# Block 2: two pairs of value projections of each layer as seven half products instead of eight

## The chip, the cores and the metric

The kernel runs on one core of a Trainium2 chip. Its measure is the device time of one execution: median 2514.1 us of three runs, from 2513.4 to 2515.23. The engines are PE (matrix multiply), DVE (vector), ACT (scalar), POOL (GpSimd) and SP, which here only issues DMAs. Each engine takes its instructions in the order written, and waits on semaphores for the others.

## The reference, cut to what matters

Two blocks run on 512 tokens of width 1024: the first ends with a feed-forward net (ffn), the second has two layers of which each computes

```
mod = c_act @ w_ada + b_ada                       # shift, scale, gate
h = rmsnorm(x, norm_w) * (1 + scale) + shift      # 512 x 1024
qa, ka, va, za, qr, kr, vr, zr, ga, gr = split(h @ w_in)
# attention: 3 patterns of 4 heads of 128; patterns 1 and 2 take keys by stride 4 and 16
o_att = softmax-weighted sum over the 3 patterns;  y_att = o_att * silu(za)
o_ret = retention(qr, kr, vr, positions);           y_ret = o_ret * silu(zr)
merged = sigmoid(ga) * (y_att @ w_proj_attn) + sigmoid(gr) * (y_ret @ w_proj_ret)
x = x + gate * (merged @ w_out)
```

va is 512 x 1536, 512 columns for each pattern; vr is 512 x 1024. The change is in how the columns of va for patterns 1 and 2, and both halves of vr, are computed from h. All is in 32-bit floats. A product of two such matrices is done as three matmuls on split operands: each matrix is kept as a high part (`h`, `wh`) and a low part (`l`, `wl`, the rest), and hi·hi, hi·lo and lo·hi are summed in PSUM.

## The kernel before

The work is one long list of TensorE matmuls of 128x128 by 128x512, and all else is arranged to have its operands there in time. A weight comes in pieces of 512 KB (128 partitions x 1024, two row blocks of 128 by 512 columns): `load_w` (L188) issues the DMA on SP into a raw tile `wr` (2 places), ACT rounds it to the high part `wh` (L144), DVE subtracts to get the low part `wl` (L145); `wh` and `wl` have 4 places each (5 where a second pool is given). A piece serves 24 matmuls: 2 row blocks, 4 blocks of 128 tokens, 3 terms. Loads are moved ahead in the instruction list by a priority offset, so SP's order is that of the loads with stores and other DMAs between them.

In block 2 `attention_v` (L959) makes the values of pattern 0 first (block of tokens by block, as soon as the norm has delivered them), and then, called inside `attention`, of patterns 1 and 2: four pieces of weight each into four PSUM banks, a copy by ACT, and 16 DMAs of 64 KB (L975) that spread each 128 tokens over four tiles by stride. The query and key projections of the 4 heads follow (`in_w_qk`), and their weights are loaded while the values are computed. `retention_v` (L1141) does the same for one half of vr, without DMAs: half 0 before retention, half 1 in its middle. `rotary_tables` (sines and cosines on DVE and ACT, L930 to L956) runs beside the first layer's strided values.

The merge loop (`rt2`, in the layer's main function) alternates weights of w_g and w_proj_ret; w_out follows. In the ffn stage a background task (`ada`) computes the modulation from 96 pieces of w_ada with DVE. Background tasks are generators: `tick()` after each group of matmuls advances them, and a number they yield is how many ticks to wait.

POOL works in the first 500 us and not after.

Of the kernel before, what the change touches and what calls it, by code (L numbers as in the profile page):

```python
# [15 lines left out]
P = 128  # L16
# [34 lines left out]
class Block:  # L51
# [136 lines left out]
    def load_w(self, src, into=None):  # L188
        with self.tc.high_priority(offset=50):
            raw = self.wp.tile([P, 1024], F32, tag="wr", name=self.nm("wr"), bufs=2)  # L190
            self.nc.sync.dma_start(out=raw, in_=src)
            if into is not None:
                self.split(*into, raw)
                return into
            self.nw += 1
            wp, n = (self.wx, 1) if self.wx and self.nw % 5 == 0 else (self.wp, 4)
            wh = wp.tile([P, 1024], F32R, tag="wh", name=self.nm("wh"), bufs=n)
            wl = wp.tile([P, 1024], F32R, tag="wl", name=self.nm("wl"), bufs=n)
            self.split(wh, wl, raw)
        return wh, wl  # L200
# [107 lines left out]

    def room(self, x):

        return [tuple(y[:, 2 * i:2 * i + 2, :].rearrange("p k q -> p (k q)") for y in (x.hi, x.lo)) for i in range(4)]
# [85 lines left out]
    def block1(self):  # L397
# [10 lines left out]
        self.nw, self.wx = 0, None  # L408
        self.wp = op(self.es, "w")
# [329 lines left out]
    def ffn(self, hf, fp, es_w):  # L739
# [5 lines left out]
        def done(i, ps):  # L745
            if i == 0:
# [4 lines left out]
                self.spawn(self.ada(pool[0], 1.2))  # L751
            if i % 2 == 0:
# [70 lines left out]
    def block2(self, h, es_w):  # L823
# [6 lines left out]
        for l in range(2):  # L830
# [7 lines left out]
            V = self.attention_v(l, h, vp, range(1))  # L838
            self.wait()
            es_w.close()  # L840
            mp, e_m = op("mrg", "right")
            mrg = [mp.tile([P, S], F32, tag="m", name=self.nm("m"), bufs=8) for _ in range(8)]
            with tc.tile_pool(name="att", bufs=1, side="right", reuse_waits="tile") as ap:
                if l == 0:
                    self.rotary_tables(ap)
                self.attention(l, h, ap, vp, V, ya, mrg)
            e_v.close()
            with tc.tile_pool(name="retv", bufs=1, side="right", reuse_waits="tile") as rv:
                W = self.retention_v(l, h, rv, 0)
# [12 lines left out]
            with tc.tile_pool(name="rt2", bufs=1, side="right", reuse_waits="tile") as rp:  # L862
                T = {}
                for i in range(11):
# [5 lines left out]
                    if c >= 0:  # L870
# [3 lines left out]
                        self.split(m.hi[:, c, :], m.lo[:, c, :], mrg[c], scale=0.5)  # L874
            e_m.close()
# [82 lines left out]

    def attention_v(self, l, h, vp, gs, V=None, ap=None):  # L959

        V = {} if V is None else V
        for g in gs:
            if g:
                for c in range(4):
                    V[g, c] = vp.tile([P, 512], F32, tag="V", name=self.nm("V"), bufs=12)

            def done(t, ps):
                if g == 0:
                    V[g, t] = vp.tile([P, 512], F32, tag="V", name=self.nm("V"), bufs=12)
                    self.nc.scalar.activation(V[g, t], ps, AF.Copy)  # L970
                    return
                x = ap.tile([P, 512], F32, tag="qk", name=self.nm("Vt"), bufs=4)
                self.nc.scalar.activation(x, ps, AF.Copy)
                for c in range(4):
                    self.nc.sync.dma_start(out=V[g, c][t * 32:t * 32 + 32, :], in_=x[c:P:4, :])  # L975

            self.T_(self.tok(h), self.A["w2_va"][l, g], 8, done, outer=0 if g else 4, ready=None if g else h.ready)
        return V

    def attention(self, l, h, ap, vp, V, ya, mrg):  # L980
# [141 lines left out]
        self.attention_v(l, h, vp, (1, 2), V, ap)  # L1122
        for hd in range(4):
            head(hd, range(3))
        self.spawn(finish(list(self.tasks)))
# [15 lines left out]
    def retention_v(self, l, h, rv, half):  # L1141
        V = []

        def done(t, ps):
            vt = rv.tile([P, 2, 512], F32R, tag="V", name=self.nm("V"), bufs=4)
            self.split(vt[:, 0, :], vt[:, 1, :], ps)
            V.append(vt)

        self.T_(self.tok(h), self.A["w2_vr"][l, half], 8, done, outer=2)
        return V  # L1150

    def retention(self, l, h, rp, rv, V, yr):
# [83 lines left out]
        Vs[1] = self.retention_v(l, h, rv, 1)  # L1236
# [417 lines left out]
```

## Time and profile before

| | us |
|---|---|
| median of 3 runs (2513.4 to 2515.23) | 2514.1 |
| profiled execution | 2515.06 |
| its span | 2513.3 |
| PE busy in the span | 2493.3 |
| DVE, ACT, POOL busy | 1403.6, 1062.7, 99.2 |

The profiled execution took 2515.06 us, of which 2513.3 lie in the span that the trace covers. The granted clock of PE is 1.0 throughout, its upper level. Approximate stages: ffn 820 to 1165 us; first layer of block 2: values 1165 to 1244, attention to 1445, values for retention to 1470, retention to 1690, merge to 1790, w_out to 1840; second layer: values to 1930, attention to 2130, and so on to the end. A view by windows says how busy each engine was in such a stage; a timeline gives single instructions with their start and length; the waits of SP are those of its DMA-issuing instructions.

### The profile page before, as it was taken

What the parts mean: (1) busy time and instruction counts of PE and PEld (TensorE: products, weight loads), DVE (VectorE), ACT (ScalarE), POOL (GpSimd) and SP (SyncE); (2) the same over time, 40 slices, a digit from 0 to 9 for tenths busy, and PEclk for the clock granted to TensorE, in tenths of its full rate; (3) what the DMA queues carried; (4) which work ended last, traced back from release to release, by engine and by line L of the source; (5) the groups of instructions that cost most, each with busy time, mean ns of one, the idle gap of its engine ahead of it and who ended that gap; (6) DMA issues with size and microseconds to landing.
All of it is one profiled execution on the core that took longest, in us unless ns stands there. A gap on an engine that the chain in (4) does not pass through costs nothing.

```text
span 2513.3 us, 31228 instructions
## 1 busy us (share of the span) xinstructions
PE 2493.3 (99%) x11850; PEld 2056.5 (82%) x11850; DVE 1403.6 (56%) x2651; ACT 1062.7 (42%) x1829; POOL 99.2 (4%) x104
## 2 busy tenths in 40 slices
PE   9999999999999999999999999999999999999998
PEld 7877777878888888888888888888888888888887
DVE  6567665776656777626333436664452343375635
ACT  4477666875334333324343432323233334233323
POOL 0023332000000000000000000000000000000000
PEclk9999999999999999999999999999999999999999
DMA  5522222323345666534422122222443222322233
GB/s 181 173 80 78 70 71 93 95 88 110 118 131 182 211 194 216 184 132 142 134 93 92 62 90 82 86 76 92 144 141 126 89 79 68 101 70 98 68 100 118
DMA packets 99129, 286.47 MB, mean 114 GB/s; under 512 B 13193, under 2 KB 19209, under 8 KB 98850
## 3 DMA queue, kind: packets, MB, share of 16 engines
q1 hardware_dynamic: 98256, 283.22, 35.2%
q8 instruction: 93, 1.52, 0.3%
q10 hardware_dynamic: 722, 1.25, 0.1%
q14 instruction: 58, 0.48, 0.1%
HBM read 259.16 MB, written 12.61 MB: 108 GB/s over the span
## 4 chain that ended last, share of the span: by engine, by line
PE 92%; DVE 3%; ACT 2%; DMA 2%; issue 1%; POOL 0%; ACTq 0%; POOLq 0%; DVEq 0%
PE ps L129 89%; PE ps L138 3%; DMA wr<-in_w_out_dram 1%; DVE wl L145 1%; ACT S L1416 1%; ACT wh L144 0%; DMA wr<-in_w_o_dram 0%; DVE yr L145 0%; POOL S L1423 0%; DVE PTl L145 0%; DVE S L1410 0%; ACT S L1421 0%; DMA x<-in_x_dram 0%; DVE xc L629 0%; DMA wr<-in_nsa_wv_dram 0%
## 5 line engine op out<-in xcount | busy, mean ns | idle before, releaser
L129 PE MATMUL ps<-h,wh 128*128 128x512 f32 (+1 forms) x4000 | 1242.8, 391 | 0.0
L129 PEld LDWEIGHTS ps<-h,wh 128*128 128x128 f32 x4000 | 733.5, 188 | 139.3 <-issue 5.1
L145 DVE TENSOR_TENSOR wl<-wr,wh 128x1024 fp32r<-128x1024 f32 x383 | 469.1, 1225 | 556.1 <-ACT wh L144 555.2
L144 ACT ACTIVATE wh<-wr 128x1024 fp32r<-128x1024 f32 x383 | 405.6, 1059 | 871.4 <-PE ps L129 658.3
L129 PE MATMUL ps<-h,wl 128*128 128x512 f32 (+1 forms) x2000 | 772.9, 386 | 0.0
L129 PEld LDWEIGHTS ps<-h,wl 128*128 128x128 f32 x2000 | 375.9, 188 | 75.7 <-DVE wl L145 0.4
L129 PE MATMUL ps<-wh,h 128*128 128x512 f32 x832 | 261.2, 392 | 0.3 <-ACT h L144 0.3
L129 PEld LDWEIGHTS ps<-wh,h 128*128 128x128 f32 x832 | 156.6, 188 | 33.6 <-DVE h L145 0.8
L129 PE MATMUL ps<-wl,h 128*128 128x512 f32 x416 | 162.4, 390 | 0.0
L129 PE MATMUL ps<-y,wh 128*128 128x512 f32 x384 | 119.3, 391 | 0.0
L129 PEld LDWEIGHTS ps<-wl,h 128*128 128x128 f32 x416 | 78.4, 188 | 16.1
L129 PE MATMUL ps<-wh,f 128*128 128x512 f32 x288 | 89.6, 389 | 0.0
L129 PEld LDWEIGHTS ps<-y,wh 128*128 128x128 f32 x384 | 71.5, 188 | 14.4
L129 PE MATMUL ps<-yr,wh 128*128 128x512 f32 x256 | 78.8, 389 | 0.0
L1416 ACT ACTIVATE S<-S,sm 128x128 f32<-128x128 f32 (+3 forms) x128 | 70.2, 550 | 19.0 <-DVE sm L1414 18.8
L1423 POOL TENSOR_SCALAR S<-S,sm 128x128 f32<-128x128 f32 (+3 forms) x64 | 69.6, 1099 | 214.0 <-ACT Q L144 78.2
L145 DVE TENSOR_TENSOR PTl<-ps,PTh 128x512 fp32r<-128x512 f32 (+1 forms) x96 | 65.0, 683 | 22.4 <-ACT PTh L144 21.6
L144 ACT ACTIVATE PTh<-ps 128x512 fp32r<-128x512 f32 (+1 forms) x96 | 56.1, 588 | 49.0 <-PE ps L138 44.0
L129 PE MATMUL ps<-y,wl 128*128 128x512 f32 x192 | 74.7, 389 | 0.0
L578 DVE SCALAR_TENSOR_TENSOR acc<-aw,cact,acc 128x512 f32<-128x512 f32 x96 | 71.8, 748 | 4.7 <-DMA acc<-in_b_ada_dram 2.7
L1014 DVE CUSTOM_DVE_ANT_0 P<-ps,c_masks 128x128 f32<-128x128 f32 (+1 forms) x96 | 31.2, 325 | 65.0 <-PE ps L129 62.9
L1410 DVE CUSTOM_DVE_ANT_0 S<-ps,c_mask 128x128 f32<-128x128 f32 (+3 forms) x128 | 59.9, 482 | 8.6 <-PE ps L129 7.5
(337 smaller groups left out, 3047.9 us busy)
## 6 DMA issues: line engine op xcount, KB each, us to landing
aw<-in_w_ada_dram SPq DMA_DIRECT2D x96, 256.0 KB, 3.9
wr<-in_w_qk_dram SPq DMA_DIRECT2D x48, 512.0 KB, 3.5
wr<-in_w_ffn_in_dram SPq DMA_DIRECT2D x44, 512.0 KB, 3.8
wr<-in_w_g_dram SPq DMA_DIRECT2D x32, 512.0 KB, 3.5
wr<-in_w_qr_dram SPq DMA_DIRECT2D x32, 512.0 KB, 3.6
wr<-in_w_mg_dram SPq DMA_DIRECT2D x24, 512.0 KB, 3.6
wr<-in_w_va_dram SPq DMA_DIRECT2D x24, 512.0 KB, 4.6
wr<-in_w_ffn_out_dram SPq DMA_DIRECT2D x22, 512.0 KB, 3.9
```

Source lines behind the costliest of these rows:

```text
L129: self.nc.tensor.matmul(out, a, b, start=start, stop=stop, skip_group_check=True)
L138: self.nc.tensor.transpose(out, in_, self.ident[:k, :k])
L144: nc.scalar.activation(hi, src, AF.Copy)
L145: nc.vector.tensor_sub(lo, src, hi.bitcast(F32))
L578: v.scalar_tensor_tensor(acc, w, self.cact[:, k:k + 1], acc, op0=ALU.mult, op1=ALU.add)
L1014: v.tensor_tensor_reduce(dst, pv, mask, 1.0, -3e38, ALU.add, ALU.max, mx[:, n:n + 1])
L1410: v.tensor_tensor_reduce(Pt[:, o], ps[:, o], self.mask[:, 512 - N:], 1.0, -3e38, ALU.add, ALU.max, mx[:, h:h + 1])
L1416: nc.scalar.activation(Ps[h], Ps[h], AF.Exp, scale=0.125, bias=nm_[:, h:h + 1], accum_out=ls[:, h:h + 1])
L1423: nc.gpsimd.tensor_scalar(Ps[h], Ps[h], r[:, h:h + 1], None, op0=ALU.mult)
```

## The change

Both pairs of products (patterns 1 and 2; both halves of vr) have the form [h · B_0 | h · B_1]. Halving tokens, rows of weight and columns gives a product of 2 by 2 blocks, and the Strassen-Winograd form of it needs 7 products of blocks instead of 8, with sums: 4 of blocks of h, 4 of blocks of weight, and 7 of results. A block product is 256 tokens x 512 rows x 512 columns: 2 pieces of weight, 12 matmuls each (2 row blocks x 2 token blocks x 3).

- `TS_` does the 7 products; three of them take original weights, four (`Tx`) take sums. The results' sums are 12 additions on DVE of 128x512, one operand in PSUM.
- `weight_sums`: four pieces of 256 KB are loaded, POOL does 4 subtractions, four DMAs store the sums to DRAM. 8 such rounds for each layer: for layer 0 in the ffn stage, for layer 1 in layer 0's merge loop, both as a background task.
- `strided_v` makes the sums of h (8 of 128x512 on DVE, 8 on POOL), splits them into high and low parts, and stores those to DRAM (8 DMAs of 512 KB), then calls `TS_` for patterns 1 and 2. `retention_v` loads the sums of h again, calls `TS_` for both halves of vr, and writes the second half to DRAM, to be loaded in the middle of retention.
- Raw weights have 4 more places in these stages, used by two of three loads. `rotary_tables` comes after the query and key projections.

```diff
     def load_w(self, src, into=None):
         with self.tc.high_priority(offset=50):
-            raw = self.wp.tile([P, 1024], F32, tag="wr", name=self.nm("wr"), bufs=2)
+            self.nr += 1
+            rp, n = (self.rawp, 4) if self.rawp and self.nr % 3 else (self.wp, 2)
+            raw = rp.tile([P, 1024], F32, tag="wr", name=self.nm("wr"), bufs=n)
...
+    def TS_(self, x, srcs, T, S_, place, done):
+        A = lambda kh, th: lambda k, t, lo: (x.l if lo else x.h)(4 * kh + k, 256 * th + t * P, 256 * th + t * P + P)
+        Sx = lambda j: lambda k, t, lo: S_(j, k, t, lo)
+        B = lambda half, kh: [srcs[half][2 * kh + i] for i in range(2)]
+        Tx = lambda j: [T[2 * j + i] for i in range(2)]
...
+        def product(b, lhs, w, start, then=None):
...
+            for i in range(2):
+                wh, wl = self.load_w(w[i])
+                for t in range(2):
+                    for kk in range(2):
...
+                        self.mm(ps, hi, wh[:, o], start and i + kk == 0, False)
+                        self.mm(ps, hi, wl[:, o], False, False)
+                        self.mm(ps, lo, wh[:, o], False, i + kk == 2)
...
+        product("a", A(0, 0), B(0, 0), True, lambda t, ps: nc.scalar.activation(e[t], ps, AF.Copy))
+        product("d", A(1, 1), Tx(3), True)
+        product("a", A(1, 0), B(0, 1), False, lambda t, ps: done(t, 0, ps))
+        product("b", Sx(1), Tx(1), True, lambda t, ps: add(u[t], e[t], ps))
+        product("c", Sx(0), Tx(0), True, p5)
+        product("b", Sx(2), Tx(2), False, p7)
+        product("a", Sx(3), B(1, 1), True, p3)
+
+    def weight_sums(self, src, dst, pool, pace):
...
+                for half, c in ((0, i), (1, i), (1, 2 + i), (0, 2 + i)):
+                    q.append(pool.tile([P, 512], F32, tag=f"q{len(q)}", name=self.nm("q"), bufs=1))
+                    self.nc.sync.dma_start(out=q[-1], in_=src[half][c][:, o])
+                yield pace[0]
+                b11, b12, b22, b21 = q
+                g.tensor_sub(b11, b12, b11)
+                g.tensor_sub(b12, b22, b12)
+                g.tensor_sub(b22, b22, b11)
+                g.tensor_sub(b21, b21, b22)
+                yield pace[1]
+                for j, t in enumerate((b11, b22, b12, b21)):
+                    self.nc.sync.dma_start(out=dst[2 * j + i][:, o], in_=t)
+                yield pace[2]
...
+    def strided_v(self, l, h, vp, V, sp):
...
+        for p in range(2):
+            for kh, th in ((1, 1), (0, 1), (0, 0), (1, 0)):
...
+                (v if th else g_).tensor_add(r.rearrange("p (k q) -> p k q", k=2), h.hi[part].bitcast(F32), h.lo[part].bitcast(F32))
...
+        for p in range(2):
+            a11, a12, a21, a22 = (R[p, kh, th] for th in range(2) for kh in range(2))
+            v.tensor_add(a22, a21, a22)
+            g_.tensor_sub(a21, a11, a21)
+            v.tensor_sub(a11, a22, a11)
+            g_.tensor_sub(a12, a12, a11)
...
+            for c in range(4):
+                nc.sync.dma_start(out=V[1 + half, c][t * 32:t * 32 + 32, :], in_=x[c:P:4, :])
...
     def retention_v(...):
+        for j in (1, 0, 2, 3):
+            H[j] = [vs.tile([P, D], F32R, tag="H", name=self.nm("H"), bufs=4) for _ in range(2)]
+            for x, y in zip(H[j], self.h_sums[j]):
+                nc.sync.dma_start(out=x.bitcast(F32), in_=y)
...
-        Vs[1] = self.retention_v(l, h, rv, 1)
+        Vs[1] = [rv.tile([P, 2, 512], F32R, tag="V", name=self.nm("V"), bufs=4) for _ in range(4)]
+        for t, x in enumerate(Vs[1]):
+            nc.sync.dma_start(out=x.rearrange("p a b -> p (a b)").bitcast(F32), in_=self.vdr[t])
```

The change also moves instructions. Three places matter below. The first is DVE in the first layer, from the last split of h (`h`) on: before, the rotary tables (`ra`, `rk`) begin there,

```order
L145 TENSOR_TENSOR h_9797<-ps_10787,h_9796 128x4x128
L145 TENSOR_TENSOR h_9797<-ps_10794,h_9796 128x4x128
L933 CAST ra<-pos 128x512
L934 TENSOR_SCALAR ra<-ra,sm_10861 128x512
L937 TENSOR_SCALAR rk<-ra 128x512
L938 TENSOR_SCALAR rk<-rk 128x512
L939 TENSOR_SCALAR rk<-rk 128x512
L944 SCALAR_TENSOR_TENSOR ra<-rk,ra 128x512 x2
L145 TENSOR_TENSOR wl_10929<-wr_10926,wh_10928 128x1024
```

and in the changed kernel the sums of h (`X`; L1075 and L1080 on DVE, of which L1082 waits for a subtraction of POOL), the splits of the sums (`H`) and those of the weights (`wl`):

```order
L145 TENSOR_TENSOR h_9927<-ps_10924,h_9926 128x4x128
L1075 TENSOR_TENSOR X_10987<-h_9926,h_9927 128x512
L1075 TENSOR_TENSOR X_10989<-h_9926,h_9927 128x512
L1075 TENSOR_TENSOR X_10995<-h_9926,h_9927 128x512
L1075 TENSOR_TENSOR X_10997<-h_9926,h_9927 128x512
L1080 TENSOR_TENSOR X_10987<-X_10989,X_10987 128x512
L145 TENSOR_TENSOR wl_11054<-wr_11051,wh_11053 128x1024
L1082 TENSOR_TENSOR X_10991<-X_10987,X_10991 128x512
L145 TENSOR_TENSOR wl_11072<-wr_11069,wh_11071 128x1024
L1080 TENSOR_TENSOR X_10995<-X_10997,X_10995 128x512
L145 TENSOR_TENSOR H_11006<-X_10991,H_11005 128x512
L145 TENSOR_TENSOR wl_11094<-wr_11091,wh_11093 128x1024
```

Up to the split of the fifth piece of weight (the first of product 3) 21 instructions stand behind the last split of h: 8 sums, 8 splits of sums, 5 of weights; the rotary tables have gone to the attention.

The second is SP in the second layer, where values (`V`) and weights (`wr`) alternate: before, the 16 stores of one pattern, four weights for queries and keys, and the 16 stores of the other,

```order
L975 DMA V_15860<-Vt_16004 32x512
L975 DMA V_15861<-Vt_16004 32x512
L191 DMA wr_16228<-in_w_qk_dram 128x1024
L191 DMA wr_16278<-in_w_qk_dram 128x1024
L191 DMA wr_16311<-in_w_qk_dram 128x1024
L191 DMA wr_16360<-in_w_qk_dram 128x1024
L975 DMA V_16010<-Vt_16138 32x512
L975 DMA V_16011<-Vt_16138 32x512
...
L975 DMA V_16013<-Vt_16156 32x512
L191 DMA wr_16393<-in_w_qk_dram 128x1024
```

and in the changed kernel two such weights, and then 24 stores in a row before the third:

```order
L193 DMA wr_16609<-in_w_va_dram 128x1024
L193 DMA wr_16655<-in_w_qk_dram 128x1024
L193 DMA wr_16688<-in_w_qk_dram 128x1024
L1098 DMA V_16254<-X_16319 32x512
L1098 DMA V_16255<-X_16319 32x512
...
L1098 DMA V_16260<-X_16322 32x512
L1098 DMA V_16261<-X_16322 32x512
L193 DMA wr_16721<-in_w_qk_dram 128x1024
L193 DMA wr_16771<-in_w_qk_dram 128x1024
```

In the first layer three weights stand ahead of the 24 stores.

The third is SP in the merge loop of the first layer: before, it holds only the weights of w_g and w_proj_ret,

```order
L191 DMA wr_14844<-in_w_g_dram 128x1024
L191 DMA wr_14876<-in_w_pr_dram 128x1024
L191 DMA wr_14912<-in_w_g_dram 128x1024
L191 DMA wr_14944<-in_w_pr_dram 128x1024
L191 DMA wr_14980<-in_w_g_dram 128x1024
L191 DMA wr_15012<-in_w_pr_dram 128x1024
```

and in the changed kernel each round of weight sums (`q` loads, `va` stores) has one or two weights between its DMAs, and they wait behind its stores:

```order
L193 DMA wr_15185<-in_w_pr_dram 128x1024
L372 DMA q_15130<-in_w_va_dram 128x512
L372 DMA q_15132<-in_w_va_dram 128x512
L372 DMA q_15134<-in_w_va_dram 128x512
L372 DMA q_15136<-in_w_va_dram 128x512
L193 DMA wr_15225<-in_w_g_dram 128x1024
L381 DMA va_15024<-q_15130 128x512
L381 DMA va_15024<-q_15134 128x512
L381 DMA va_15024<-q_15132 128x512
L381 DMA va_15024<-q_15136 128x512
L193 DMA wr_15269<-in_w_pr_dram 128x1024
```

## Rows read from the trace of the kernel before

**Rows 1.** The page: busy time by engine, and the chain by engine

```profile
PE 2493.3 (99%) x11850; PEld 2056.5 (82%) x11850; DVE 1403.6 (56%) x2651; ACT 1062.7 (42%) x1829; POOL 99.2 (4%) x104
...
PE 92%; DVE 3%; ACT 2%; DMA 2%; issue 1%; POOL 0%; ACTq 0%; POOLq 0%; DVEq 0%
```

**Rows 2.** Windows by stage: ffn, attention, merge, w_out, values of the second layer

```profile
core 0: us, PE busy (x) PEld busy (x) DVE busy (x) ACT busy (x) POOL busy (x), PEclk, DMA share, GB/s
820.00:1050.00 230.00, 230.00 (x1091) 193.66 (x1090) 171.93 (x226) 81.03 (x111) 0.00 (x0) 1.00 0.63 204
1245.00:1400.00 155.00, 155.00 (x720) 127.09 (x719) 50.40 (x136) 61.91 (x150) 0.00 (x0) 1.00 0.30 95
1690.00:1790.00 100.00, 100.00 (x463) 83.33 (x462) 44.66 (x71) 28.38 (x38) 0.00 (x0) 1.00 0.28 90
1800.00:1850.00 50.00, 49.02 (x228) 40.32 (x227) 34.74 (x54) 19.59 (x29) 0.00 (x0) 1.00 0.66 224
1885.00:1930.00 45.00, 45.00 (x201) 37.08 (x200) 10.52 (x17) 16.95 (x28) 0.00 (x0) 1.00 0.40 140
```

**Rows 3.** Timeline (start, length, us) of PE: transposes, and 48 matmuls later

```profile
1191.54 1.03 PE L138 MATMUL ps<-ident,xn 128*128 128x128 f32 x8
1192.33 0.48 PE L129 MATMUL ps<-wh,h 128*128 128x512 f32 x1
...
1195.37 0.39 PE L129 MATMUL ps<-wl,h 128*128 128x512 f32 x1
...
1206.25 0.39 PE L129 MATMUL ps<-wl,h 128*128 128x512 f32 x1
```

**Rows 4.** Timeline of DVE, the end of the norm before the first values

```profile
1192.80 1.29 DVE L145 TENSOR_TENSOR h<-ps,h 128x512 fp32r<-128x512 f32 x2 [3.85 <-ACT h L144]
1194.01 0.42 DVE L933 CAST ra<-pos 128x512 f32<-128x512 int32 x1
```

**Rows 5.** Costliest groups of the page: line, engine, operation, count, busy, mean ns

```profile
L145 DVE TENSOR_TENSOR wl<-wr,wh 128x1024 fp32r<-128x1024 f32 x383 | 469.1, 1225 | 556.1 <-ACT wh L144 555.2
L144 ACT ACTIVATE wh<-wr 128x1024 fp32r<-128x1024 f32 x383 | 405.6, 1059 | 871.4 <-PE ps L129 658.3
L145 DVE TENSOR_TENSOR PTl<-ps,PTh 128x512 fp32r<-128x512 f32 (+1 forms) x96 | 65.0, 683 | 22.4 <-ACT PTh L144 21.6
L144 ACT ACTIVATE PTh<-ps 128x512 fp32r<-128x512 f32 (+1 forms) x96 | 56.1, 588 | 49.0 <-PE ps L138 44.0
```

**Rows 6.** Tile yraw: duration of a POOL addition, minimum, median and maximum ns

```profile
L1474 POOL TENSOR_TENSOR yraw<-Z,W x16: 725/732/1658, 145.7 to 434.3; 64x256 f32<-64x256 f32 x16
```

**Rows 7.** Timeline from 236.8 us, DVE and POOL side by side

```profile
236.90 1.22 DVE L145 TENSOR_TENSOR wl<-wr,wh 128x1024 fp32r<-128x1024 f32 x1
237.06 1.66 POOL L1474 TENSOR_TENSOR yraw<-Z,W 64x256 f32<-64x256 f32 x1 [2.76 <-DMA W<-Z]
```

**Rows 8.** Timeline from 222.9 us, DVE and POOL side by side

```profile
223.22 0.73 POOL L1475 TENSOR_TENSOR yraw<-Z,W 64x256 f32<-64x256 f32 x1
...
223.26 1.78 DVE L145 TENSOR_TENSOR wl<-wr,wh 128x1024 fp32r<-128x1024 f32 x1
```

**Rows 9.** POOL by line and shape from 190 to 510 us, mean ns

```profile
L1423 POOL TENSOR_SCALAR S<-S,sm 128x512 f32<-128x512 f32 x14 | 22.7, 1634 | 20.8 <-ACT ma L1276 7.3 <-DVE Pc L1437 6.9 <-DVE sm L1418 6.2
...
L1423 POOL TENSOR_SCALAR S<-S,sm 128x256 f32<-128x256 f32 x12 | 10.9, 924 | 19.7 <-ACT Z L1470 8.7 <-PE ps L129 5.7 <-DVE sm L1418 5.2
```

**Rows 10.** Timeline of the DMA queue SP, second layer: issues joined in stretches

```profile
1887.05 10.03 SPq L975 DMA_DIRECT2D V<-Vt  x16
1897.18 10.28 SPq L191 DMA_DIRECT2D wr<-in_w_qk_dram  x4
```

**Rows 11.** Line 975, the stores of strided values: issue time in ns

```profile
L975 SPq DMA_DIRECT2D V<-Vt x64: 472/592/1661, 1221.8 to 1918.3; - x64
```

**Rows 12.** DMA issues of the page: count, size, median us to landing

```profile
aw<-in_w_ada_dram SPq DMA_DIRECT2D x96, 256.0 KB, 3.9
wr<-in_w_qk_dram SPq DMA_DIRECT2D x48, 512.0 KB, 3.5
```

More of the change, by code (lines that the diff above doesn't have):

```diff
@@ L309, in room, with all_weight_sums @@
+    def all_weight_sums(self, l, pool, pace):
+        A = self.A
+        for n, src in (("va", [A["w2_va"][l, g] for g in (1, 2)]), ("vr", [A["w2_vr"][l, g] for g in range(2)])):
+            self.w_sums[n, l] = self.dp.tile([8, P, D], F32, tag=f"{n}{l}", name=f"{n}{l}")
+            yield from self.weight_sums(src, self.w_sums[n, l], pool, pace)
     def room(self, x):
@@ L837, in block2 @@
             vp, e_v = op("attv")
-            V = self.attention_v(l, h, vp, range(1))
+            V = self.attention_v(l, h, vp)
             self.wait()
             es_w.close()
+            with tc.tile_pool(name="sv", bufs=1, side="right", reuse_waits="tile") as sp:
+                self.rawp = sp
+                self.strided_v(l, h, vp, V, sp)
+                self.rawp = None
             mp, e_m = op("mrg", "right")
@@ L956, in rotary_tables, with attention_v, done @@
         nc.scalar.activation(self.cos, k, AF.Sin)
[L959 to L977, printed above, removed]
-        return V
+    def attention_v(self, l, h, vp):
+        V = {}
+        def done(t, ps):
+            V[0, t] = vp.tile([P, 512], F32, tag="V", name=self.nm("V"), bufs=12)
+            self.nc.scalar.activation(V[0, t], ps, AF.Copy)
+        self.T_(self.tok(h), self.A["w2_va"][l, 0], 8, done, outer=4, ready=h.ready)
+        return V
@@ L1138, in attention, with retention_v, done @@
         self.wait()
[L1141 to L1149, printed above, removed]
+    def retention_v(self, l, h, rv, vs):
+        nc = self.nc
+        self.vdr = self.dp.tile([4, P, D], F32, tag="vdr", name=self.nm("vdr"))
+        V = [rv.tile([P, 2, 512], F32R, tag="V", name=self.nm("V"), bufs=4) for _ in range(4)]
+        H = {}
+        for j in (1, 0, 2, 3):
+            H[j] = [vs.tile([P, D], F32R, tag="H", name=self.nm("H"), bufs=4) for _ in range(2)]
+            for x, y in zip(H[j], self.h_sums[j]):
+                nc.sync.dma_start(out=x.bitcast(F32), in_=y)
+        def done(t, half, z):
+            if half == 0:
+                self.split(V[t][:, 0, :], V[t][:, 1, :], z)
+                return
+            y = vs.tile([P, 2, 512], F32R, tag="Y", name=self.nm("Y"), bufs=3)
+            self.split(y[:, 0, :], y[:, 1, :], z)
+            nc.sync.dma_start(out=self.vdr[t], in_=y.rearrange("p a b -> p (a b)").bitcast(F32))
+        self.TS_(h, [self.A["w2_vr"][l, i] for i in range(2)], self.w_sums["vr", l],
+                 lambda j, k, t, lo: H[j][lo][:, k * 256 + t * P:k * 256 + t * P + P],
+                 lambda: vs.tile([P, S], F32, tag="X", name=self.nm("X"), bufs=6), done)
         return V
```

66 lines of the change are left out of this document (62 added, 4 removed).

## The prediction

> **What bounds the kernel now.** I read the page's busy times first, then its chain, then windows by stage, and then timelines at the places that the change touches. The page should show the reader one full engine: PE is busy 99% of the span, and 92% of the chain that ended last is PE's [rows 1]. The windows say that this holds stage by stage: PE is busy 230.00 of 230.00 us in the ffn, 155.00 of 155.00 in attention, 100.00 of 100.00 in the merge, 45.00 of 45.00 in the second layer's values, at a granted clock of 1.00 [rows 2]. So a matmul taken out is worth its whole pitch, and nothing that other engines get costs anything until a matmul waits for it. The other engines have room: DVE is busy 10.52 and ACT 16.95 of those 45 us, and POOL nothing [rows 2]. What the change can lose, it loses as waits of PE that are not there now.
>
> **The gain.** 48 matmuls start between 1195.37 and 1206.25 us [rows 3], 10.88 / 48 = 0.2267 us each. A pair of products takes 2 x 96 = 192 matmuls (8 row blocks, 4 token blocks, 3 terms); seven half products take 7 x 24 = 168. There are 2 pairs in each of 2 layers: 4 x 24 = 96 matmuls, 96 x 0.2267 = 21.8 us. A stage of seven products lasts 168 x 0.2267 = 38.1 us, one product 5.44.
>
> **What is added beside PE.** Each stage loads 14 pieces of weight instead of 8, each good for 12 matmuls (2.72 us) instead of 24. A piece costs ACT 1.059 and DVE 1.225 us [rows 5], which keeps up with 2.72. In a strided stage DVE has 14 x 1.225 = 17.2 for these, and 28 instructions of 128x512 (8 sums of h, 8 splits of them, 12 sums of results) at 0.683 from the row of the same size [rows 5], 19.1: 36.3 us of work in 38.1. DVE goes from a quarter busy to nearly full, so the cover that now hides its work is gone there, and the order of its queue decides. I walked it at the places where a matmul waits.
>
> Sums of h. The last two splits of h end at 1192.80 + 1.29 = 1194.09 [rows 4]. Behind them stand 21 instructions up to the split that product 3 needs: 16 x 0.683 + 5 x 1.225 = 17.1, done at 1211.2. PE reaches product 3 after the transposes at 1192.33 [rows 3] and 39 + 48 matmuls, 1212.05. That is 0.9 us early, if POOL, which makes four subtractions between them, costs DVE nothing. The trace does not have POOL's 128x512 subtraction. Its 64x256 addition takes 0.732 [rows 6]; the one-operand operation goes from 924 to 1634 ns between 256 and 512 columns [rows 9], a fixed part of about 0.21, so I estimate 0.21 + 2 x 0.52 = 1.25 us. And the two engines do not run side by side on such work: a 64x256 addition of POOL that began 0.16 us after a weight split of DVE took 1.66 instead of 0.73 [rows 7], and a split that began 0.04 us after POOL's addition took 1.78 instead of 1.22 [rows 8]. Four subtractions at 1.25 would put the split 5.0 later, 4.1 us too late; with none of it the price is nothing. Some fall where DVE waits for ACT or for POOL's result anyway. I take 2 us for each layer, 4 in all.
>
> A page of the Trainium skill says the same against this change: GPSIMD Engine Reference, Specifications, has POOL's SBUF interfaces shared with VectorE, in contention with DVE instructions that have two SBUF inputs. The trace agrees (1.66 for 0.73, 1.78 for 1.22). By the rule taken whole, each subtraction stops DVE for its length, and the sum would be 4.1 us a layer instead of my 2.
>
> Product 6. Its first weight is issued behind 8 stores of values, which wait for product 3 (16.3 us into the stage, and a copy of ACT, 0.588 [rows 5]). Stores take 0.592 each to issue [rows 11], so it goes out at about 22, lands 3.5 later [rows 12] and is ready for DVE at 26.6. In the first layer DVE's split of it stands behind two additions that need the end of product 5 (27.2): 27.2 + 0.7 + 1.2 = 29.1, and PE wants it at 27.7: 1.5 us. In the second layer the split stands between these additions: 0.3.
>
> Queries and keys. The last 24 stores of values cannot begin before product 6's first result and its additions (about 34.2 into the stage) and then hold SP for 24 x 0.592 = 14.2 us, to 48.4; 16 of them take 10.03 us now [rows 10]. What is queued behind them is the next weight: 48.4 + 0.33 + 3.5 + 1.06 + 1.22 = 54.5 until its low half is there. In the second layer only two weights are ahead of the stores; they feed 48 matmuls, to 38.1 + 10.9 = 49.0, and PE wants the low half two matmuls on: 5 us. Before, four such weights went out between two blocks of stores [rows 10]. In the first layer three are ahead, to 54.4, but there ACT has to empty a bank at 54.4 before it can round the weight (0.588 + 1.059, then DVE's 1.225), while PE has under 1 us of other work: 2 us.
>
> Retention's values. No stores by stride, the first pieces are loaded during attention, and the sums of h come back by 8 loads. The one for product 6 is freed by product 4, 5.4 us ahead, against 3.5 to land: 0.5 a layer, 1 in all, between 0 and 4.
>
> Weight sums in the ffn: 32 subtractions x 1.25 = 40 us of POOL, and DVE is busy 171.93 of 230 [rows 2], so even if all of it excluded DVE, 212 of 230. DMA stands at a share of 0.63 there [rows 2]. Weights are split 4 places ahead (20 us). Nothing, up to 3.
>
> Weight sums in the merge. A round is a load, four dependent subtractions, stores, and the next loads wait for those: about 3.5 + 5.0 + 3 + 0.6 = 12.1 us, 13 with a wait for DVE. The weights of the merge stand between the rounds' DMAs on SP. Eight rounds; the second piece of w_out stands behind the last stores, 8c - 2.5 us after the first loads, and needs 5.8 to be split. PE wants it 480 matmuls later, less the transposes, about 107.3. So the wait is 8c - 104: nothing up to c = 13, 8 us at 14. I take 1.
>
> Rotary tables go beside attention, where DVE is busy 50.40 of 155 [rows 2]: nothing. The reload of retention's second half is 229 matmuls (52 us) ahead of its use: nothing.
>
> **Sum.** Back: 4 + 1.8 + 7 + 1 + 1 = 14.8. Net -21.8 + 14.8 = -7.0. The profiled execution took 2515.06, 1.0 above the median of the runs; 2515.1 - 7.0 = 2508.1, and on the median's footing 2507.1.
>
> **Rivals.**
> 1. Nearly all of it is kept: POOL's subtractions fall into DVE's gaps, stores issue at the fastest 472 ns [rows 11], which takes 2.9 off both waits for query weights. Back about 4 (0 and 2 for these, 1.5 for product 6, 0.5 for the rest): -17.8, 2496.3 or a little above. For it: the splits are 0.9 us early on paper. Against: the two overlaps above, and that the median issue is 592.
> 2. The gain goes, to within 0.2%: the DMA engines are full in the value stages. A strided stage moves 14 pieces and 8 sums of 512 KB and 32 stores of 64 KB, 13.6 MB in 38.1 us, 357 GB/s. The fullest stretch has 224 GB/s at a share of 0.66 [rows 2], 339 for a share of 1: 40.1 us, 2 us a stage, four stages 8, beside the 14.8: +1.0, 2515. Against it: some pieces are loaded ahead of the stage. The Trainium skill (DMA: Bandwidth & Descriptors, Specifications) has about 358 GB/s for HBM per core; by that figure, 38.0 us, this term would be nothing. No stretch here reaches a share of 1, so it stays open.
> 3. Slower: the merge's rounds. If a round takes 15 us (a subtraction at 1.66 like the collided one [rows 7] and a load at 3.9 [rows 12] under load would do), SP holds w_out's weights back and PE waits 8 x 15 - 104 = 16 us, in place of my 1: +8, 2522. It decides for slower from c = 14.5. For it: all four subtractions depend on each other, and SP has one queue. Against: PE's weights there are 20 us ahead at the start.
>
> **Chances.** Forecast 0.46, rival 1 0.22, rival 2 0.22, rival 3 0.10. A measurement of this kernel can tell about 0.2%, 5 us, from no change, so faster is below 2509.1: rival 1 and four fifths of the forecast's own spread (2502 to 2512), 0.59, rounded to 0.60; same is the rest of it and rival 2, 0.31; slower 0.09. The range of 8 in 10 reaches into rival 1 and over rival 2: 2497 to 2517.
>
> **What would show it.** 96 fewer matmuls of 128x512. PE idle for some us before product 3 and 6 in both strided stages, and before the third weight for queries in the second layer, with a row of 24 stores on SP ahead of it. Weight splits of DVE longer than 1.225 where POOL works. A round of POOL in the merge under 13 us and no idle PE there; 15 or more would prove rival 3. I am wrong if PE stays busy through the strided stages, or if the waits lie elsewhere (ffn, attention, retention).

## The result, and the profile after

The changed kernel takes 2527.6 us (median of 6 runs, 2525.7 to 2531.8) against 2514.7 for the kernel before (6 runs, 2513.4 to 2516.8): ratio 1.0053, 95% interval 1.0044 to 1.0063. It is 13 us slower. I had forecast 7 us faster, with 2517 as the upper end. The profiled execution took 2531.82, 4.2 above the median; its span is 2530.0, which is 16.7 more than the span before. The figures by stage below are of this execution.

The page of the changed kernel, lines that answer to [rows 1, 5]: busy times by engine, the chain by engine, and the weight splits.

```profile
PE 2484.5 (98%) x11754; PEld 2040.3 (81%) x11754; DVE 1514.0 (60%) x2755; ACT 1097.0 (43%) x1868; POOL 229.3 (9%) x184
...
PE 25%; DMA 2%; DVE 2%; ACT 1%; issue 0%; SPq 0%; POOL 0%; ACTq 0%; DVEq 0%; POOLq 0%
...
L145 DVE TENSOR_TENSOR wl<-wr,wh 128x1024 fp32r<-128x1024 f32 x407 | 511.9, 1263 | 484.9 <-ACT wh L144 483.8
```

The 96 matmuls are gone (11,850 to 11,754). PE's busy time fell by only 8.8 us though, not by 21.8, while the span grew: part of PE's busy time is now slower matmuls. The chain's shares add up to about 30%, so it was not followed to the start, and its 25% can't be set against the 92% of before. The average weight split of DVE grew by 0.04 us, which says nothing of where. The windows do, by three stages of [rows 2] and three more (columns as there):

```profile
820.00:1050.00 230.00, 230.00 (x1093) 193.81 (x1092) 189.91 (x226) 82.03 (x111) 50.19 (x32) 1.00 0.82 277
1195.00:1235.00 40.00, 37.24 (x162) 29.82 (x161) 29.95 (x33) 20.86 (x27) 7.64 (x4) 1.00 0.65 233
1245.00:1400.00 155.00, 153.00 (x706) 124.62 (x705) 54.60 (x145) 61.85 (x149) 0.00 (x0) 1.00 0.32 104
1690.00:1790.00 100.00, 100.00 (x462) 83.37 (x461) 43.53 (x62) 22.64 (x31) 44.74 (x28) 1.00 0.64 215
1790.00:1840.00 50.00, 39.01 (x144) 27.80 (x143) 26.86 (x33) 15.45 (x19) 6.64 (x4) 0.93 0.69 229
1935.00:1950.00 15.00, 9.87 (x32) 7.30 (x33) 6.10 (x13) 4.36 (x5) 0.00 (x0) 0.77 0.46 157
```

The ffn and the merge up to 1790 us lose nothing. The 50 us behind the merge, where w_out is multiplied, have 11.0 us of idle PE and a granted clock of 0.93; before, such a stretch was busy 49.02 of 50 at 1.00 [rows 2]. The second large hole is at 1935 us. To size both, the starts of the same matmul in the two traces are compared, with 0.2267 us added for each matmul that the changed kernel has left out up to there; the table says by how much this difference grows in each stage:

| stage | forecast, us | measured, us |
|---|---|---|
| strided values and first queries, layer 0 (sums of h, product 6, query weights) | 5.5 | 6.7 |
| attention, layer 0 (rotary tables) | 0 | 2.2 |
| retention's values, layer 0 | 0.5 | 2.0 |
| **merge and w_out, layer 0 (weight sums)** | **1** | **16.2** |
| strided values, layer 1 | 2.3 | 2.1 |
| query weights, layer 1 | 5 | 8.7 |
| attention and the rest, layer 1 | 0.5 | 0.0 |
| sum | 14.8 | 38.0 |

Ahead of the ffn the two traces already differ by 0.5 us. 38.0 and this 0.5, less the 21.8 of the matmuls, give the 16.7 by which the spans differ. The expectations of the experiments put the merge's loss at 16.4, by a coarser sum over the stages.

What happens at w_out is read on two engines. First the DMA queue SP of the changed kernel, from the last round's loads on (`q`, loads; `vr`, stores; `wr`, weights):

```profile
1787.74 1.83 SPq L372 DMA_DIRECT2D q<-in_w_vr_dram  x4
1789.62 0.42 SPq L193 DMA_DIRECT2D wr<-in_w_out_dram  x1
1794.51 5.63 SPq L381 DMA_DIRECT2D vr<-q  x4
1800.24 16.55 SPq L193 DMA_DIRECT2D wr<-in_w_out_dram  x5
...
1821.12 3.51 SPq L193 DMA_DIRECT2D wr<-in_w_out_dram  x2
```

and the same weights in the kernel before:

```profile
1765.84 34.51 SPq L191 DMA_DIRECT2D wr<-in_w_out_dram  x6
```

Before, four of these six pieces went out at 1765.84, 1771.68, 1776.71 and 1782.57, 30 to 14 us before PE's first matmul of w_out (1796.11); the other two followed at 1798.88 and 1800.02. Now the first goes out at 1789.62 and the next at 1800.24, behind the last store of the last round. Then PE, whose w_out starts at 1798.5 (idle time before a matmul in brackets, with its releaser):

```profile
1805.60 0.50 PE L129 MATMUL ps<-wh,mo 128*128 128x512 f32 x1 [1.41 <-ACT wh L144]
1806.86 0.50 PE L129 MATMUL ps<-wl,mo 128*128 128x512 f32 x1 [0.76 <-DVE wl L145]
...
1813.11 0.49 PE L129 MATMUL ps<-yr,mo 128*128 128x512 f32 x1 [0.74 <-ACT yr L144]
1815.35 4.37 PE L129 MATMUL ps<-yr,mo 128*128 128x512 f32 x11 [1.75 <-DVE yr L145]
...
1827.52 0.49 PE L129 MATMUL ps<-wh,mo 128*128 128x512 f32 x1 [1.75 <-ACT wh L144]
1828.78 0.50 PE L129 MATMUL ps<-wl,mo 128*128 128x512 f32 x1 [0.77 <-DVE wl L145]
```

The first two pieces of w_out feed 24 matmuls each; behind them six pieces are wanted one after another for the first block of tokens, 6 matmuls each. They can come no faster than two raw places let them, and every one is late. The engines' order adds to it. The third piece, issued at 1800.72, is split only at 1812.02 (`yr`): ACT comes to it behind the last splits of the merge's result (`mo`), these wait for DVE's sums (`T`, `m`), and those stand in DVE's line behind the split of the late second piece, for which DVE waited 5.24 us:

```profile
1805.58 1.23 DVE L145 TENSOR_TENSOR wl<-wr,wh 128x1024 fp32r<-128x1024 f32 x1 [5.24 <-ACT wh L144]
...
1807.32 0.68 DVE L963 SCALAR_TENSOR_TENSOR T<-T,ps 128x512 f32<-128x512 f32 x1
...
1811.48 0.63 ACT L147 ACTIVATE mo<-m 128x512 fp32r<-128x512 f32 x1 [2.08 <-DVE m L964]
1812.02 1.99 ACT L144 ACTIVATE yr<-wr 128x1024 fp32r<-128x1024 f32 x2
```

Between 1790 and 1834 PE's idle times add up to 11.0 us, 10.0 more than in the same place before; the other 6.1 are matmuls that take longer: the eleven from 1815.35 on take 4.37 us where 2.5 is their pitch, and each start after a wait costs some 0.2 more than the wait.

The hole at 1935 us is the one forecast for the third query weight of layer 1. SP:

```profile
1912.86 5.03 SPq L193 DMA_DIRECT2D wr<-in_w_qk_dram  x2
1919.52 15.12 SPq L1098 DMA_DIRECT2D V<-X  x24
1934.74 8.14 SPq L193 DMA_DIRECT2D wr<-in_w_qk_dram  x4
```

PE at the same place:

```profile
1940.09 1.22 PE L129 MATMUL ps<-h,wh 128*128 128x512 f32 x2 [5.60 <-ACT wh L144]
...
1941.94 1.05 PE L129 MATMUL ps<-h,wh 128*128 128x512 f32 x2
1942.79 0.63 PE L129 MATMUL ps<-h,wl 128*128 128x512 f32 x1
```

The 24 stores take 15.1 us (forecast 14.2) and PE waits 5.60 (forecast 5). Then come matmuls at 0.425 us each (1941.94 to 1942.79, two of them), about twice the pitch; full speed is back near 1948. These cost another 3 us that I had not counted.

### The profile page after: what moved, and what is told of

It reads as the page before. It is cut to its first block, busy times and chain, and to the rows that moved or that the text cites. A ratio compares the mean times of both kernels' runs of the same rounds, so it can differ in the third digit from the quotient of the medians.

```text
span 2530.0 us, 31670 instructions
## 1 busy us (share of the span) xinstructions
PE 2484.5 (98%) x11754; PEld 2040.3 (81%) x11754; DVE 1514.0 (60%) x2755; ACT 1097.0 (43%) x1868; POOL 229.3 (9%) x184
## 3 DMA queue, kind: packets, MB, share of 16 engines
q10 hardware_dynamic: 722, 1.25, 0.1%
## 5 line engine op out<-in xcount | busy, mean ns | idle before, releaser
L145 DVE TENSOR_TENSOR wl<-wr,wh 128x1024 fp32r<-128x1024 f32 x407 | 511.9, 1263 | 484.9 <-ACT wh L144 483.8
L144 ACT ACTIVATE wh<-wr 128x1024 fp32r<-128x1024 f32 x407 | 429.2, 1058 | 803.2 <-PE ps L129 481.1
L129 PE MATMUL ps<-wh,h 128*128 128x512 f32 x512 | 161.4, 392 | 0.0
L375 POOL TENSOR_TENSOR q<-q,q 128x512 f32<-128x512 f32 x16 | 25.4, 1586 | 1046.0 <-DMA q<-in_w_va_dram 952.4
L129 PEld LDWEIGHTS ps<-wh,h 128*128 128x128 f32 x512 | 96.3, 188 | 20.7 <-DVE h L145 0.8
L129 PE MATMUL ps<-wl,h 128*128 128x512 f32 x256 | 100.6, 393 | 1.8 <-DVE wl L145 1.7
L660 DVE SCALAR_TENSOR_TENSOR acc<-aw,cact,acc 128x512 f32<-128x512 f32 x96 | 78.1, 814 | 8.0 <-DMA aw<-in_w_ada_dram 4.4
L129 PE MATMUL ps<-wh,H 128*128 128x512 f32 x256 | 80.3, 391 | 1.8 <-DMA H<-hsums 1.5
```

The source lines that it names most:

```text
L129: self.nc.tensor.matmul(out, a, b, start=start, stop=stop, skip_group_check=True)
L144: nc.scalar.activation(hi, src, AF.Copy)
L145: nc.vector.tensor_sub(lo, src, hi.bitcast(F32))
L375: g.tensor_sub(b11, b12, b11)
L660: v.scalar_tensor_tensor(acc, w, self.cact[:, k:k + 1], acc, op0=ALU.mult, op1=ALU.add)
```

## Experiments

Times are medians, each against the kernel before in the same series of runs (2514.6 to 2515.2 us). The changed kernel, which was not run again beside them, stands at ratio 1.0053. Losses by stage are from the matched starts, as in the table above.

**Where the sums are made.** The weight sums of layer 1 are moved from the merge into layer 0's retention; for want of space they are done in 16 rounds of 256 columns.

```diff
-                    self.spawn(self.all_weight_sums(1, rp, (3.0, 6.5, 3.0)))
...
+            self.spawn(self.all_weight_sums(1, rp, (5.0, 6.0, 5.0), 256))
```

> The second layer's weight sums are made in the first layer's retention (in pieces of half the width, 16 rounds for 8, since no more memory is free there) and not in the merge loop. Theory A: the loss at the merge and w_out, 16.4 us against before, comes from weights that stand behind the rounds of sums on SP, just where w_out comes next and nothing is loaded ahead. With about 200 us for the rounds it is gone: about 2511 us, no idle PE and no lower clock around 1800 us. Theory B: it comes from what the rounds load the DMA engines and the shared port with, wherever they stand: then retention has waits of its own, and the time is 2520 or more.

Measured: 2545.2 us, ratio 1.0121 (1.0106 to 1.0136), slower still, and in theory B's range. The idle time in w_out is gone but for 0.54 us, and retention has a new one, 19.4 us in all. The longest piece: between 1590.10 and 1610.41 SP issues no weight, only loads and stores of the sums, and PE waits. First SP:

```profile
1590.10 0.41 SPq L193 DMA_DIRECT2D wr<-in_w_qr_dram  x1
...
1610.41 0.42 SPq L193 DMA_DIRECT2D wr<-in_w_qr_dram  x1
```

Then PE:

```profile
1616.76 0.79 PE L129 MATMUL ps<-rh,rh 128*128 128x512 f32 x1 [10.54 <-ACT rh L144]
```

So moving the rounds moves the wait with them, which SP's order would do, and so would what the rounds do on POOL and in the transfers. The next run and one further down tell these apart.

**The queue of the sums.** Loads and stores of the sums, in the merge as in the changed kernel, are issued on POOL's queue.

```diff
-                    self.nc.sync.dma_start(out=q[-1], in_=src[half][c][:, o])
+                    g.dma_start(out=q[-1], in_=src[half][c][:, o])
...
-                    self.nc.sync.dma_start(out=dst[2 * j + i][:, o], in_=t)
+                    g.dma_start(out=dst[2 * j + i][:, o], in_=t)
```

> The DMAs of the weight sums are issued by POOL and not by SP, rounds, places and bytes as in the changed kernel. Theory A (order on SP): the weights of the merge and of w_out no longer wait behind the stores; the loss of 16.4 us falls to 3 or less, about 2513 us. Theory B (bytes or port): rounds take the same 13 us at a DMA share of 0.65, and 10 us or more of the loss stay: 2521 or more.

Measured: 2517.3 us, ratio 1.0007 (0.9998 to 1.0017), 10 us less than the changed kernel, and between the two theories' times. The place decides for theory A: the merge and w_out lose 2.6 us here instead of 16.2. The rounds are slower, not faster (14.7 us from first load to first load), and the last one's stores go out up to 1807.6, well after w_out has begun (1794.27). But SP issues w_out's weights from 1764.00 on, as before the change:

```profile
1764.00 34.51 SPq L193 DMA_DIRECT2D wr<-in_w_out_dram  x6
```

Two waits of 1.26 and 0.76 are left in w_out, and one of 1.10 behind it.

**The engine of the merge's subtractions.** They go to DVE; the DMAs stay on SP. (The first number that `weight_sums` yields is 7.0 in the ffn and 3.0 in the merge, so the ffn's subtractions stay on POOL. These numbers are microseconds by the program's own count of matmul time, not ticks.)

```diff
-        g = self.nc.gpsimd
+        g = self.nc.gpsimd if pace[0] > 5 else self.nc.vector
```

> In the merge loop the subtractions of the weight sums run on DVE and not on POOL (the ffn's stay on POOL). A round has four of them in series, about 1.6 us each on POOL with its waits for DVE; at 0.69 a round falls from 13.4 to about 10 us. Theory A: by 8 rounds x c the last weights are then in time, the merge's loss falls from 16.4 to 4 or less: about 2514. Rival: a round is set by its loads and stores, not by POOL: rounds stay over 12 us and the loss over 10: 2522 or more.

Measured: 2512.6 us, ratio 0.9992 (0.9983 to 1.0001), 15 us less than the changed kernel. From the tile `q` (duration in ns, minimum, median and maximum), first in the changed kernel and then here:

```profile
L375 POOL TENSOR_TENSOR q<-q,q x8: 1287/1572/2117, 1698.9 to 1792.9; 128x512 f32<-128x512 f32 x8
```

```profile
L375 DVE TENSOR_TENSOR q<-q,q x8: 683/693/695, 1694.2 to 1769.6; 128x512 f32<-128x512 f32 x8
```

A round now takes 10.5 us (first loads of the first at 1689.89, of the eighth at 1763.53, seven rounds between), and four pieces of w_out go out between 1763.95 and 1779.38, ahead of its first matmul at 1792.93. SP from the third piece on, and the window of w_out:

```profile
1773.67 23.50 SPq L193 DMA_DIRECT2D wr<-in_w_out_dram  x4
```

```profile
1790.00:1840.00 50.00, 49.60 (x226) 40.58 (x225) 34.26 (x51) 18.59 (x25) 0.44 (x1) 1.00 0.62 211
```

A shorter round and another queue each take most of the loss away, and they have one thing in common: SP is free when w_out's weights are due. How long a round lasts mattered mainly through SP: with rounds of 14.7 us on POOL's queue the stage loses 2.6 us, with 13.4 on SP's 16.2. Another spacing of the rounds (the numbers yielded) was not tried.

**One round more.** The eighth round is done twice.

```diff
-        for i in range(2):
-            for o in (slice(0, 512), slice(512, D)):
+        last = dst is self.w_sums.get(("vr", 1))
+        for r in (0, 1, 2, 3, 3) if last else range(4):
+            i, a = r // 2, r % 2 * 512
+            for o in (slice(a, a + 512),):
```

> The changed kernel with one round more in the merge: the eighth round of weight sums is done a second time (same data, same place), so nine rounds of 13.4 us stand ahead of w_out's weights. Theory A (the 16.4 us lost in merge and w_out are the rounds that still run when w_out begins, since SP holds the weights behind their stores): the ninth round comes wholly after that point and makes the loss longer by most of a round, 8 to 13 us less what two weights issued inside it cover; 2536 to 2541. Theory B (the loss is spread over the merge: POOL's subtractions and the transfers slow weight splits and loads everywhere, one ninth more of it for one round more): 16.4 / 8 = 2 us more, 2529.6.

Measured: 2531.9 us, ratio 1.0070 (1.0055 to 1.0085). That is 4.3 us more than the changed kernel with overlapping intervals, between what the two theories said, and by the time alone it decides nothing. SP shows why the size is off: a second and a third piece of w_out go out inside the ninth round, ahead of its stores.

```profile
1797.99 0.38 SPq L193 DMA_DIRECT2D wr<-in_w_out_dram  x1
...
1799.37 0.70 SPq L193 DMA_DIRECT2D wr<-in_w_out_dram  x1
1805.14 5.93 SPq L383 DMA_DIRECT2D vr<-q  x4
1811.17 6.77 SPq L193 DMA_DIRECT2D wr<-in_w_out_dram  x3
```

The merge and w_out lose 22.0 us against 16.2 in the changed kernel, and before 1790 PE is never idle for 0.4 us in either. The place is theory A's; the price of a late round, about 6, is below the 8 to 13 that I had put on it.

**Retention again, on the other queue.** The kernel of the first experiment, with the sums' DMAs on POOL's queue (the same two lines as above).

> The kernel that made the second layer's weight sums in retention (16 rounds of 256 columns; 2545.2 us), with the loads and stores of the sums issued on POOL's queue instead of SP's. Theory A (there too it was SP's order: retention's weights stood behind rounds, 15.9 us once): SP is free, the waits of retention go, and since the merge holds no rounds its 16.4 us are gone as well; 2527.6 - 16.4 = 2511, up to 2516 if POOL's own work in retention comes late by its queue. Theory B (the sums disturb retention by what they do on POOL, in POOL's turns with DVE and in the transfers, on whichever queue): 2535 or above.

Measured: 2517.7 us, ratio 1.0011 (1.0002 to 1.0021), 27 us less than with SP and close to theory A's range, 1.7 above it. PE's idle time in retention falls from 19.4 to 1.9 us, and the 10.54 us wait has become the one below, so it had come from SP's order and not from POOL's work or the transfers.

```profile
1599.16 0.50 PE L129 MATMUL ps<-rh,rh 128*128 128x512 f32 x1 [0.84 <-ACT rh L144]
```

**The stores of strided values.** First all on POOL's queue.

```diff
-                nc.sync.dma_start(out=V[1 + half, c][t * 32:t * 32 + 32, :], in_=x[c:P:4, :])
+                g_.dma_start(out=V[1 + half, c][t * 32:t * 32 + 32, :], in_=x[c:P:4, :])
```

> The 64 KB stores of the strided values (line 1098) are issued by POOL and not by SP. Theory A: the 5.6 us wait for the third query weight in the second layer, and the half-speed stretch of about 3 us behind it, come from the 24 stores ahead of that weight on SP; both go, and 1 to 2 us in the first layer: 2516 to 2518 us. Rival: the weight would be late anyway, since DVE or ACT have its split behind other work: within 2 us of the changed kernel.

Measured: 2519.4 us, ratio 1.0015 (1.0006 to 1.0025), 8 us less than the changed kernel and 1.4 above theory A's range. The waits of product 6 and of the third query weight are gone, and a new one has come, since the places of the values (`X`) become those of queries and keys (`qk`) and have to be stored first:

```profile
1934.02 1.57 PE L129 MATMUL ps<-qk,qk 128*128 128x128 f32 x4 [3.94 <-ACT qk L1152]
```

Then together with the subtractions on DVE:

> Two edits at once that were each run alone: the merge's subtractions on DVE (15.0 us less than the changed kernel) and the stores of strided values on POOL's queue (8.2 less). Theory A, the two waits are separate (w_out's weights behind the rounds of the merge; the second layer's third query weight behind 24 stores): the gains add, 2527.6 - 15.0 - 8.2 = 2504.4, some 10 us under the kernel before, and no idle time of PE over 1 us in the merge. Theory B, one wait hides the other or SP's later order gives one back: 2510 to 2513, like the better edit alone. Either way the wait of PE for qk's place near 1934 us (3.94 with these stores on POOL's queue) should stay, since 24 stores still stand in one queue.

Measured: 2502.4 us, ratio 0.9952 (0.9939 to 0.9966). The gains add, to within 2 us, and the wait for `qk` stays with 3.83 us. Then the stores alternately on both queues:

```diff
+                (nc.sync if c % 2 else g_).dma_start(out=V[1 + half, c][t * 32:t * 32 + 32, :], in_=x[c:P:4, :])
```

> The merge's subtractions on DVE, and the stores of strided values alternately on SP's and POOL's queue: 12 of the last 24 on each, 12 x 0.59 = 7.1 us instead of 14.2. Theory A (the third query weight of the second layer is late only by the length of the row of stores ahead of it on SP, and the place of qk by the row on POOL): both waits, 5.6 here or 3.94 there, go to nothing, because 7.1 us less than 14.2 exceeds both; 2504.4 - 3.9 = 2500.5. Theory B (the stores are slow by what they move, not by their queue: 24 DMAs of 64 KB with rows by stride share the same DMA engines): the last store lands at the same time and a wait of 3 us or more stays; 2504 or above.

Measured: 2499.3 us, ratio 0.9940 (0.9927 to 0.9952). Both waits are gone, as theory A said, and theory B's wait of 3 us does not come. SP's row is half as many stores in two thirds of the time (15.1 us for 24 before), so the length of the row belongs at least in part to the queue. How much the shorter row did for the third query weight this run can't tell, since that weight now stands ahead of the row on SP (three at 1887.39, where the changed kernel has two). The windows of w_out and of the second layer's values and queries are nearly full:

```profile
1887.39 8.02 SPq L193 DMA_DIRECT2D wr<-in_w_qk_dram  x3
1896.40 10.13 SPq L1098 DMA_DIRECT2D V<-X  x12
```

```profile
1790.00:1840.00 50.00, 49.16 (x223) 39.98 (x222) 34.33 (x50) 18.59 (x25) 1.66 (x1) 1.00 0.61 211
1890.00:1930.00 40.00, 40.00 (x181) 32.63 (x180) 22.04 (x37) 16.21 (x24) 6.41 (x12) 1.00 0.55 169
```

This version is 15 us faster than the kernel before and 28 faster than the changed one.

**The rotary tables** after the products at attention's end (stores on two queues):

```diff
-        if l == 0:
-            self.rotary_tables(ap)
         self.spawn(finish(list(self.tasks)))
...
+        if l == 0:
+            self.rotary_tables(ap)
         self.wait()
```

> As the kernel with stores on two queues, and the rotary tables of the first layer are made after the 12 products of attention's end instead of before them. Theory A (the 1.4 us that PE waits near 1411 us for ACT's copy t, and some of the 2.0 us lost in attention, come from the table loads of ACT, 1.28 each, that sine and cosine put ahead of that copy): that idle time goes, 1.5 to 2 us less than the kernel without this edit. Theory B (the tables then stand before the split of the attention's last results or the first values of retention): the wait moves to 1440 to 1475 us and the time is the same or up to 2 us longer.

Measured: 2501.3 us, ratio 0.9945 (0.9933 to 0.9958), not told apart from 2499.3. The wait for ACT's copy `t` (1.40) went, and two others came in attention for the next thing that ACT copies, `PT`. In time, theory B was right; in place, neither. Ahead of the first of the two ACT loads a table all the same (1406.99, 1.28 us, for `m`): the edit moved the loads and did not save them.

```profile
1409.42 1.13 PE L129 MATMUL ps<-PT,V 128*128 128x256 f32 x4 [1.26 <-ACT PT L1202]
1430.14 1.13 PE L129 MATMUL ps<-PT,V 128*128 128x256 f32 x4 [1.26 <-ACT PT L1202]
```

**All sums of h on DVE** (stores on two queues; `g_` becomes `v` in three lines of `strided_v`):

> As the kernel with stores on two queues, and the eight sums of h that POOL made in each layer are made by DVE. Theory A (DVE and POOL take turns at these operations, so POOL's 1.29 to 2.1 each costs DVE as much or more than the 0.68 that DVE needs itself): the waits for weight splits of product 3 and 6 in the first layer's strided values (1.09 and 1.47 in the changed kernel) fall to about 0 to 1 together, 1 to 2 us less over both layers. Theory B (they run side by side well enough, and DVE's queue is what is full, 36 us of work in 38): 8 x 0.68 = 5.4 us more on DVE before product 3 makes PE wait 2 to 4 us longer in each layer, 4 to 8 us more.

Measured: 2500.1 us, ratio 0.9941 (0.9928 to 0.9953), the same as 2499.3 within the intervals. Theory B, 4 to 8 us slower, falls, and theory A's 1 to 2 us less do not show either. Product 3's split in layer 0 is late by 0.24 us instead of 1.13, and a wait of 0.54 for ACT has come ahead of it:

```profile
1209.63 0.50 PE L129 MATMUL ps<-wh,h 128*128 128x512 f32 x1 [0.54 <-ACT X L356]
1216.17 0.50 PE L129 MATMUL ps<-wl,h 128*128 128x512 f32 x1 [0.24 <-DVE wl L145]
```

By the starts of matmuls the first layer's seven products lose 2.2 us here and 1.9 with POOL's help, so the smaller wait of product 3 gave nothing back. Eight more operations of DVE are as cheap as sharing them.

## Why the prediction was wrong

**The step that failed is "Weight sums in the merge"**, which took 1 us for a loss of 16.2. That is 15 of the 23 us by which all losses exceed their forecast. The length of a round was somewhat too low: 12.1 to 13 forecast, 13.4 measured (first loads at 1693.66, the eighth's at 1787.74). POOL's subtraction alone was as estimated (1.29 against 1.25), but its median in the merge is 1.5 to 1.7, through the turns that it takes with DVE. At 13.4 the formula 8c - 104 gives 3.2, and for what it describes it was nearly right: the second piece of w_out cost 1.41 + 0.76 = 2.2 us. What it left out is larger. It priced the first late weight and took the rest of w_out to follow in time. But the last six of its eight pieces are wanted close together. In the kernel before, four pieces had gone out when PE reached w_out, and the eighth went out 11 us later (1807.17). With SP held to 1800 us one piece had gone out, and the eighth followed 26 us after PE's first matmul of w_out (1824.30 against 1798.51). The lead of the whole series was gone, not just of one piece, and DVE and ACT, which work in order, were held by the late pieces too. Of the 11.0 us of idle time 1.2 fall on the last piece of w_proj_ret (1792), 2.2 on the second piece of w_out and 7.6 on the later ones, and 6.1 more are the slower matmuls behind these waits.

**Rival 3** named the place, the queue and the engine. That its 16 us are what the stage lost is luck: they came from a round of 15 us and one late weight, and the round was 13.4, at which its formula gives 3.2. Its condition (c from 14.5) was wrong for the same reason as the step above, so the rival, which I gave 0.10, was priced too low.

**Query weights.** The mechanism was right in the second layer: 15.1 us of stores for 14.2, a wait of 5.60 for 5. The matmuls at half speed behind it were not counted (3 us). In the first layer, waits of 0.70 at 1263 and 1.31 at 1285 stand for the forecast 2; the first is for a weight's split, the second for a result of DVE (`mc`) that stands in its line behind such a split.

**Product 6** was right in layer 0 (1.46 us at 1232.98 for 1.5). **Product 3** waits 1.09 behind the sums of h, for the 2 us taken. In layer 1 they wait 0.81 and 0.45, for 0.3 and 2. DVE and POOL do take turns there, as in [rows 7, 8]; the timeline of the changed kernel:

```profile
1203.69 1.61 POOL L1081 TENSOR_TENSOR X<-X,X 128x512 f32<-128x512 f32 x1 [0.69 <-DVE X L1080]
1204.07 2.31 DVE L145 TENSOR_TENSOR wl<-wr,wh 128x1024 fp32r<-128x1024 f32 x1
...
1206.91 2.39 DVE L145 TENSOR_TENSOR H<-X,H 128x512 fp32r<-128x512 f32 x2
...
1207.07 1.68 POOL L1083 TENSOR_TENSOR X<-X,X 128x512 f32<-128x512 f32 x1 [1.76 <-DVE X L1082]
```

A split of 1.225 took 2.31. The rule quoted ahead (the Trainium skill, GPSIMD Engine Reference, Specifications) is borne out in direction, but the 4.1 us that it would have cost, taken whole, were not lost: part of POOL's time fell into DVE's own wait for POOL's result (1.18 us at 1200.01).

**Rotary tables** were put at nothing because DVE has room in attention. The wait came from ACT, which I had not looked at: sine and cosine make it load tables (1.28 us each, the cosine's at 1408.94), and the copy `t` that PE needs stands behind them (1410.77). That is 1.4 of the 2.2 us, and it went when the tables were moved.

**Retention's values:** mechanism as forecast (product 6's `H` from DRAM), 1.50 us in the first layer for 0.5. In the experiments the same wait varies from nothing to 1.35, so this term differs from one execution to the next. **The ffn sums** cost nothing, as forecast: 230.00 of 230.00 us, though the DMA share went from 0.63 to 0.82.

**Rival 2** (full DMA engines) did not happen: the strided stage has a share of 0.65. **Rival 1** (2496) is near the run in which the two queue waits are taken away: 2499.3.

In short, the arithmetic of the gain held, and what it was lost to is order on one queue. All DMAs with a wait in front stand in one line on SP, so a store that waits for POOL, or 24 stores in a row, hold up weights that need nothing from them. A page of the Trainium skill (DMA: Bandwidth & Descriptors, Anatomy of one DMA — SWDGE (gpsimd) path) says where such a wait is: a wait on a semaphore happens at the issuing sequencer, before dispatch. The runs with the sums on POOL's queue agree (10 us and 27 us less by the queue alone).

What stays open: why the ninth round cost 6 and not 8 to 13 us, beyond the three pieces that went out early, and in which stage the 4.2 us lie by which the profiled execution exceeds the median.

## What to carry to other kernels

When work is put between prefetches on one DMA queue, ask not only when the first weight behind it comes, but how much lead the whole series behind it had and needs; price the loss of the lead, not of one load. Background traffic that waits for a slow engine belongs on a queue where nothing urgent stands behind it, and a row of small stores can be split over two. And where a chain of dependent operations sets how long a queue is held, the faster engine can be worth more than the idle one: DVE's 0.69 for POOL's 1.3 to 2.2 was worth 15 us here, though DVE had 44 us of other work in those 100 and POOL none.

## What the runs showed of the hardware

Idle time of PE was dearer than its length. In the run with the sums in retention, retention lost 30.1 us against the changed kernel with 19.4 of idle time, and the stretch with the end of its longest wait (1610 to 1620 us) shows a granted clock of 0.56. Windows of the changed kernel (the figure after POOL's is the granted clock):

```profile
1810.00:1820.00 10.00, 7.36 (x24) 4.94 (x22) 6.40 (x10) 4.21 (x5) 0.00 (x0) 0.83 0.32 100
...
1830.00:1840.00 10.00, 9.59 (x37) 7.42 (x36) 6.18 (x11) 2.75 (x5) 0.00 (x0) 0.84 0.89 299
...
1940.00:1950.00 10.00, 9.87 (x32) 7.30 (x33) 6.10 (x13) 3.21 (x4) 0.00 (x0) 0.71 0.38 124
```

Behind the 5.60 us hole the granted clock is 0.71, a mixture of the upper level (2.4 GHz) and the lower (1.2), and the matmuls there run at 0.425 us. In w_out, within a series of waits of 0.7 to 1.8 us, it is 0.83 and 0.84. Around and behind a single wait of 1.46 at 1232.98 (1230 to 1250) it stays at 1.00. What the clock fell short of 1.00 comes to 1.7 + 1.6 + 2.9 = 6.2 us in these three windows, as an estimate of its price a sixth of all that was lost. The Trainium skill (TensorE: Matmul & The Clock Gate, Part 1) describes a gate with these two levels; the pitch there, 0.425 us against 0.2267, is nearly doubled and agrees.

The transfers had more room than I feared: the ffn ran at 277 GB/s and a share of 0.82 without a wait of PE.
